# A trunk layer with sixteen experts on one core: two weight parts read one stage earlier, a table read early, the last sums of squares regrouped

## The chip, the core and the metric

The kernel runs on one NeuronCore of a Trainium2 chip. Its metric is the time that the device takes for one execution, in microseconds. A core has five engines with a queue each: TensorE (PE in the profile; PEld is its weight load), VectorE (DVE), ScalarE (ACT), GpSimd (POOL) and SyncE (SP), which here only issues DMA transfers. The engines wait for each other by semaphores.

## The reference

A sequence of 2048 positions of 1024 numbers, all float32, passes one layer. A mixer (three groups of heads side by side, each normalised, then one output product) is added to the input. Then a mixture of experts is added, and the sum is normalised:

```
h = x + mixer(x)
e = two experts of 16 for each position          # best group of four, then best two inside it
y = sum over the two of gate * (silu(xn @ w_gate[e]) * (xn @ w_up[e])) @ w_down[e]   # xn = rms_norm(h)
out = rms_norm(h + y) * final_norm_g
```

An expert's `w_gate` and `w_up` are 1024 x 512, its `w_down` 512 x 1024.

## The kernel before

Products are done in three passes: every float32 operand is split into a rounded high part and the rest, and high x high, high x low and low x high are summed (the three matmuls in a row of each kind).

`phases12` computes the mixer and the routing. A small scheduler written in Python (`Flow`) sets the order of its work when the program is built. The mixer's output product runs over two halves of the positions, each in four chunks of 256 columns; a chunk's split weights lie in a tile `w` of a pool with two buffers, 4416 float32 wide, chunk after chunk. In the fourth chunk (`m == 3`) SP stores every finished tile of h twice, to `hd` and to `hc`. `route` then chooses the experts and sorts the (position, expert) pairs into blocks of 128 of one expert. Its tables (which expert and which ring slots a block uses, how many blocks an expert has, the number of blocks `nb`, the last block `nl`) lie in `tab`.

`moe` runs the blocks. Its engines have an explicit program each, and start together behind a barrier. There are 42 blocks in this run.

- An expert's weights are six parts of 1 MB, numbered over all experts from 0 to 95: parts 0 to 3 of an expert hold gate and up columns, parts 4 and 5 the down rows. SP reads part n into a raw buffer (`raw(n)`). VectorE splits it into one of nine slots of `ring` (L1600 or L1598 the high halves, L1618 or L1616 the low ones), then counts `s_w`. Parts 0 and 1 lie in `stg`, two buffers that `route` fills (L1330) while the mixer ends. Parts 2 to 5 are read after the barrier into slots 6 and 7 of the ring, which are not yet in use. All later parts use the two buffers of `stg` in turn, and the read of part n waits until part n - 2 is split:

```
for n in range(NST, 96):
    if n == 4:
        sp.wait_ge(p_q, 2)
    if n >= 6:
        sp.wait_ge(s_w, n - NST + 1 if n > 7 else n - 5)
```

- TensorE, in step b: reads three numbers of the table (`load`, L1673), multiplies gate and up of block b (L1692, 24 matmuls for each half f of the 512 columns, which wait for the part's `s_w`), transposes the product of block b - 1 (`th`) and the input of block b + 1 (`tx`), both at L1699, and does the down product of block b - 1 (L1731 to L1733). Before the first step it runs 16 and 6 transposes that compute nothing (`warm`, L1666). After the last step it reads three numbers again (L1771, at a place that depends on `nl`) and does the last down product.
- ScalarE moves results out of PSUM, applies silu (`glu`, L1813 and L1814, into `hs` and `hu`), and computes each finished block's normalisation (`newton`, L1860 and on).
- GpSimd gathers a block's rows (L1892), multiplies hs by hu (`hm`, L1910), adds a block's output to `hd` (L1896), reads finished rows back (L1900), multiplies them by `gf` (L1945; `gf` itself is scaled once at L1930) and stores them (L1904).
- The end: after the last step GpSimd copies two index columns (L1951), does a tiny operation (L1955) and reads back the rows of the last two blocks into `ze[0]` and `ze[1]`. VectorE adds the last down product to `ze[0]` in two halves (L1643), ScalarE sums squares in four halves (L1887), first both of `ze[1]`, then both of `ze[0]`, and VectorE turns the sums into factors (from L1645) and scales.

Of the kernel before, what the change touches and what calls it, by code (L numbers as in the profile page):

```python
# [9 lines left out]
F32 = mybir.dt.float32  # L10
F32R = mybir.dt.float32r
# [8 lines left out]
P = 128  # L20
S = 2048
D = 1024
# [122 lines left out]
def phases12(tc, io, hd, hc, tab, gcol, ident, c8, stg):  # L145
# [5 lines left out]
    with ctx:  # L151
# [6 lines left out]
        wp = pool("w", 2)  # L158
# [42 lines left out]
        def wgen():  # L201
            for n in range(len(chunks)):
                raws = load_w_raw(n)
                yield
                while begun[0] < n - 1:
                    yield
                w = wp.tile([P, 2, 8, 276], F32R, name="w")
                for k in range(0, 8, 2):
                    rw_ = raws[k // 4][:, k % 4:k % 4 + 2, :]
                    for j in range(2):  # L210
                        g = col(chunks[n][2], k + j)
                        A.activation(w[:, 0, k + j, 0:256], rw_[:, j], AF.Copy, scale=g)  # L212
                    for j in range(2):
                        stt(w[:, 1, k + j, 0:256], rw_[:, j], col(chunks[n][2], k + j), w[:, 0, k + j, 0:256].bitcast(F32), OP.mult, OP.subtract)
                    yield
                if n in routed:
                    while "rw" not in done:
                        yield
                    G.tensor_copy(w[:, 0, :, 256:276], routed[n])
                    tt(w[:, 1, :, 256:276], routed[n], w[:, 0, :, 256:276].bitcast(F32), OP.subtract, G)  # L220
                wt[n] = w
                if 6 <= n < 14:
                    yield from route_w(n - 6)
                if n == 2:
                    yield from spatial_w()
            done.add("w")
# [859 lines left out]
        def route():  # L1086
# [240 lines left out]
            while stg is not None and len(stg) < NST:  # L1327
                t = c8.tile([P, 2048], F32, name="stg", tag="c8")
                for o, i in stage(io, t, len(stg)):
                    nc.sync.dma_start(out=o, in_=i)  # L1330
                stg.append(t)
# [163 lines left out]
def moe(tc, io, hd, hc, out, tab, gcol, ident, stg):  # L1495
# [5 lines left out]
    with ctx:  # L1501
# [3 lines left out]
        ring = mp.tile([P, RING, 2, 2048], F32R, name="ring")  # L1505
        xg = mp.tile([P, 2, D + 16], F32, name="xg")
        sc = mp.tile([P, 48, 2], F32, name="sc")
# [4 lines left out]
        yb = mp.tile([P, 2, D], F32, name="yb")  # L1512
        gf = mp.tile([P, D], F32, name="gf")
        idf = mp.tile([P, 48], I32, name="idf")
        nw = mp.tile([P, 12], F32, name="nw")
# [4 lines left out]
        ew = mp.tile([P, 6, 2], F32, name="ew")  # L1520
# [9 lines left out]
        s_er = [S_("er%d" % i) for i in range(4)]  # L1530

        raw = lambda n: ring[:, 6 + (n - 2) // 2, n % 2].bitcast(F32) if 2 <= n < 6 else stg[n % NST]
# [25 lines left out]
        with tc.tile_critical():  # L1558
            with nc.Block() as blk:
                @blk.sync  # L1560
                def _(sp):
                    sp.wait_ge(p_q, 1)
                    for n in range(NST, 96):
                        if n == 4:
                            sp.wait_ge(p_q, 2)
                        if n >= 6:
                            sp.wait_ge(s_w, n - NST + 1 if n > 7 else n - 5)
                        if n == RING:
                            sp.dma_start(out=gf, in_=io["final_norm_g"].unsqueeze(0).to_broadcast((P, D))).then_inc(s_gf, 16)
                        for o, i in stage(io, raw(n), n):  # L1570
                            sp.dma_start(out=o, in_=i).then_inc(s_er[n - 2] if n < 6 else s_st[n % NST], 16)

                @blk.vector
                def _(v):
                    nhi = nha = 0
                    for n in range(96):
# [67 lines left out]
                    v.wait_ge(s_es, 4)  # L1644
# [17 lines left out]
                def _(t):  # L1662
                    def warm(n):

                        for _ in range(n):
                            t.transpose(pd[0][:, 0:P], ident, ident)  # L1666
# [78 lines left out]
                    def step(b):  # L1745
                        m = load(b)
# [24 lines left out]
                    m = [t.value_load(meta[0:1, ds(nl * 3 + j, 1)], min_val=0, max_val=(90 if j == 0 else RING - 3)) for j in range(3)]  # L1771
                    t.wait_ge(s_hm, nl * 2 + 2)
                    t.wait_ge(a_ht, nl)
                    th()
                    t.wait_ge(s_hlo, 1)
                    t.wait_ge(a_y, nl)
                    down(m)

                @blk.scalar
                def _(a):  # L1780
# [64 lines left out]
                    def newton(f):  # L1845
# [9 lines left out]
                        if f == 0:  # L1855
                            a.wait_ge(p_k, 3)
                            a.wait_ge(p_q, 1)
# [18 lines left out]
                    if 3 in AH:  # L1876
                        a.wait_ge(s_er[1], 32)
                        hi(3, range(4))
                    chain(a, nb, 0, NBMAX, step)
                    n = 0  # L1880
                    for i in (1, 0):
                        for h in range(2):
                            a.wait_ge(s_zl if i == 0 else s_e[i], 1 + h if i == 0 else 16)
                            if n:
                                a.wait_ge(s_es, n)
                            n += 1
                            a.activation(pj, ze[i][:, h * 512:(h + 1) * 512], AF.Square, accum_out=es[:, h, i:i + 1]).then_inc(s_es, 1)  # L1887

                @blk.gpsimd
                def _(g):  # L1890
# [26 lines left out]
                    g.memset(cmag, float(0x1EF759DF)).then_inc(p_k, 1)  # L1917
                    nb = g.value_load(meta[0:1, 159:160])
# [5 lines left out]
                    g.tensor_copy(nw[:, 7:8], c15).then_inc(p_q, 1)  # L1924

# [24 lines left out]
                    for i in range(2):  # L1950
                        g.tensor_copy(idg[:, i:i + 1], idf[:, ds(nl - i, 1)]).then_inc(p_c, 1)  # L1951
# [4 lines left out]
                    for i in range(2):  # L1956
                        back(ze[i], idg[:, i:i + 1], s_e[i])
                    for i in range(2):
                        g.wait_ge(s_v, fin_v[0] - 1 + i)
                        store(ze[i], idg[:, i:i + 1])  # L1960
# [3 lines left out]
def trunk(tc, io, out):  # L1964
    nc = tc.nc
    with tc.tile_pool(name="outer", bufs=1) as po, tc.tile_pool(name="c8", bufs=2) as c8, tc.tile_pool(name="odr", bufs=1, space=DRAM) as pd:
# [7 lines left out]
        phases12(tc, io, hd, hc, tab, gcol, ident, c8, stg)  # L1974
# [26 lines left out]
```

## Time and profile before

| | us |
|---|---|
| median of 3 runs | 1590.1 |
| the three runs | 1586.15, 1590.1, 1593.86 |
| profiled execution | 1590.12 |
| its span, first to last instruction | 1588.3 |
| TensorE busy | 1489.4 (94% of the span) |
| VectorE busy | 976.4 (61%) |
| ScalarE busy | 865.6 (54%) |
| GpSimd busy | 484.6 (31%) |

The mixer's output product ends about 737 us from the start of the span, the routing about 762 us, and the blocks' steps run from there to about 1553 us. A share of busy time is an average over these stages. What sets the end is read from the chain of waits and from each engine's timeline at the start, in the first steps and at the end of the experts' stage.

### The profile page before, as it was taken

The page shows a single profiled execution, that of the slowest core. Times are in us where ns is not written, and L with a number is a line of the kernel's source. Part 1 is how long each engine was busy: PE and PEld are TensorE (multiplying, and loading weights), DVE is VectorE, ACT ScalarE, POOL GpSimd, SP SyncE. Part 2 cuts the span into 40 slices and gives each one's busy share as a digit, 9 for nine tenths or more (in the row PEclk, how much of TensorE's full clock was granted, in tenths as well). Part 3 has the DMA queues.
Part 4 walks back from the last instruction along what each step waited for, and adds up shares of the span by engine and source line. Part 5 has one row for each costly group of instructions (what it writes and reads, how often), then busy time and mean ns, then how long its engine had stood idle before and what let it go on. Part 6 is the DMA issues. An engine that isn't in the chain of part 4 may idle for free.

```text
span 1588.3 us, 25588 instructions
## 1 busy us (share of the span) xinstructions
PE 1489.4 (94%) x8373; PEld 1283.5 (81%) x8374; DVE 976.4 (61%) x2009; ACT 865.6 (54%) x1915; POOL 484.6 (31%) x400
## 2 busy tenths in 40 slices
PE   7998989999999999996899899999999999999993
PEld 6776888878899989996688678888888888888882
DVE  6588752664642678888888876577888858203001
ACT  6368544687454444311346456665666665666662
POOL 0132000000000000010355545655555555455442
PEclk9999988999999999998899999999999999999996
DMA  6247733213633627607678887778888877434342
GB/s 179 69 80 142 208 104 120 93 54 93 188 99 104 236 81 263 241 27 267 215 226 241 259 253 198 214 214 264 272 222 236 261 220 204 126 75 107 90 116 74
DMA packets 212862, 267.46 MB, mean 168 GB/s; under 512 B 34808, under 2 KB 177344, under 8 KB 212736
## 3 DMA queue, kind: packets, MB, share of 16 engines
q1 hardware_dynamic: 187792, 201.95, 40.3%
q0 software_dynamic: 24672, 62.80, 16.3%
q8 instruction: 78, 1.28, 0.3%
q10 hardware_dynamic: 272, 1.05, 0.2%
q14 instruction: 48, 0.39, 0.1%
HBM read 217.09 MB, written 76.94 MB: 185 GB/s over the span
## 4 chain that ended last, share of the span: by engine, by line
PE 74%; DVE 13%; DMA 4%; ACT 4%; issue 2%; POOL 1%; SPq 0%; DVEq 0%; POOLq 0%; ACTq 0%
PE pg L1692 24%; PE z L90 8%; PE z L92 8%; PE z L91 8%; PE pd L1733 4%; PE pd L1732 4%; PE pd L1731 4%; DMA stg<-in_expert_w_up_dram 3%; DVE ring L1600 2%; PE pt L1699 2%; DVE ring L1618 2%; DVE ht L171 1%; DVE w L171 1%; PE m L924 1%; DVE xT L169 1%
## 5 line engine op out<-in xcount | busy, mean ns | idle before, releaser
L1692 PE MATMUL pg<-ring,xs 128*128 x2016 | 488.3, 395 | 9.7 <-DVE ring L1618 8.0
L1692 PEld LDWEIGHTS pg<-ring,xs 128*128 128x128 f32 x2016 | 378.2, 189 | 89.7 <-issue 11.8
L90 PE MATMUL z<-w,xT 128*128 128x256 f32 (+1 forms) x848 | 250.4, 295 | 5.6 <-DVE ht L171 3.8
L92 PE MATMUL z<-w,xT 128*128 128x256 f32 (+1 forms) x848 | 244.9, 289 | 6.9 <-DVE xT L169 6.9
L91 PE MATMUL z<-w,xT 128*128 128x256 f32 (+1 forms) x848 | 244.6, 288 | 0.0
L1600 DVE TENSOR_SCALAR ring<-stg,gcol 128x512 fp32r<-128x512 f32 x242 | 130.9, 602 | 169.8 <-PE pg L1692 86.7
L1618 DVE SCALAR_TENSOR_TENSOR ring<-stg,gcol,ring 128x512 fp32r<-128x512 f32 x248 | 213.9, 923 | 0.0
L90 PEld LDWEIGHTS z<-w,xT 128*128 128x128 f32 x848 | 164.3, 194 | 9.0 <-issue 5.1
L92 PEld LDWEIGHTS z<-w,xT 128*128 128x128 f32 x848 | 164.1, 194 | 8.2 <-DVE xT L169 8.2
L91 PEld LDWEIGHTS z<-w,xT 128*128 128x128 f32 x848 | 164.5, 194 | 1.4 <-issue 1.4
L1731 PE MATMUL pd<-ring,hh 128*128 x336 | 131.4, 391 | 1.7 <-DVE hh L1637 1.7
L1896 POOL DMA_INDIRECT hd<-yb,tab x41 | 77.5, 1891 | 177.8 <-ACT yb L1835 177.8
L1733 PE MATMUL pd<-ring,hh 128*128 x336 | 131.2, 390 | 0.0
L1732 PE MATMUL pd<-ring,hh 128*128 x336 | 131.2, 390 | 0.0
L1910 POOL TENSOR_TENSOR hs<-hs,hu 128x256 f32<-128x256 f32 x84 | 106.5, 1268 | 50.1 <-ACT hu L1814 47.8
L1945 POOL TENSOR_TENSOR yb<-yb,gf 128x1024 f32<-128x1024 f32 x40 | 116.2, 2905 | 4.7 <-ACT hu L1860 4.7
L171 DVE SCALAR_TENSOR_TENSOR w<-raw,vec,w 128x256 fp32r<-128x256 f32 x176 | 82.0, 510 | 55.4 <-ACT w L212 55.4
L212 ACT ACTIVATE w<-raw,vec 128x256 fp32r<-128x256 f32 x176 | 77.1, 497 | 60.8 <-PE z L92 36.7
L90 PE MATMUL z<-xT,w 128*128 128x512 f32 x256 | 109.8, 429 | 0.2 <-ACT xT L312 0.2
L171 DVE SCALAR_TENSOR_TENSOR ht<-z,rsd,ht 128x256 f32<-128x256 f32 x176 | 85.1, 484 | 30.1 <-PE z L92 22.2
L91 PE MATMUL z<-xT,w 128*128 128x512 f32 x256 | 101.5, 396 | 0.2 <-DVE xT L169 0.2
L92 PE MATMUL z<-xT,w 128*128 128x512 f32 x256 | 101.3, 396 | 0.0
(441 smaller groups left out, 2573.2 us busy)
## 6 DMA issues: line engine op xcount, KB each, us to landing
stg<-in_expert_w_gate_dram SPq DMA_DIRECT2D x62, 512.0 KB
stg<-in_expert_w_up_dram SPq DMA_DIRECT2D x62, 512.0 KB
stg<-in_expert_w_down_dram SPq DMA_DIRECT2D x60, 512.0 KB
raw<-in_w_in_dram SPq DMA_DIRECT2D x48, 256.0 KB
raw<-in_w_out_dram SPq DMA_DIRECT2D x24, 512.0 KB
ht<-in_x_dram SPq DMA_DIRECT2D x16, 512.0 KB
yp<-yTd SPq DMA_DIRECT2D x8, 1024.0 KB
hd<-ht SPq DMA_DIRECT2D x16, 512.0 KB
```

The lines of the kernel that those rows point to most:

```text
L90: nc.tensor.matmul(ps, ah, bh, start=first, stop=False)
L91: nc.tensor.matmul(ps, ah, bl, start=False, stop=False)
L92: nc.tensor.matmul(ps, al, bh, start=False, stop=last)
L171: stt = lambda o, a, s, b, o0, o1: V.scalar_tensor_tensor(out=o, in0=a, scalar=s, in1=b, op0=o0, op1=o1)
L1600: x = v.tensor_scalar(out=ring[:, r, 0, sl], in0=src[:, sl], scalar1=g, scalar2=None, op0=OP.mult)
L1618: x = v.scalar_tensor_tensor(out=ring[:, r, 1, sl], in0=src[:, sl], scalar=g, in1=hi, op0=OP.mult, op1=OP.subtract)
L1692: i = t.matmul(pg[f], xx[j // 2], w[j % 2], start=k == 0 and j == 0, stop=k == 7 and j == 2)
L1731: t.matmul(pd[n], hh[:, 0, kf], w[0], start=kf == 0, stop=False)
L1732: t.matmul(pd[n], hh[:, 0, kf], w[1], start=False, stop=False)
L1733: i = t.matmul(pd[n], hh[:, 1, kf], w[0], start=False, stop=kf == 3)
L1910: g.tensor_tensor(out=o, in0=o, in1=hu[:, f * 256:(f + 1) * 256], op=OP.mult).then_inc(s_hm, 1)
L1945: g.tensor_tensor(out=z, in0=z, in1=gf, op=OP.mult).then_inc(p_z, 1)
```

## The change

It has three parts.

1. The pool of `w` is parted into two pools of one buffer, one of them (`we`) opened outside, so that its memory lives on. When the last chunk of the mixer begins (`h == 1 and m == 3`), the buffer of the chunk before the last is free. ScalarE's queue then issues four transfers that read parts 2 and 3 into it. In `moe`, parts 2 and 3 are taken from there (`early`), parts 4 and 5 are read into ring slot 7, SP begins with part 4, and its wait for `p_q` of 2 is gone. The same memory is later cut into `yb`, `gf`, `hs`, `hu` and small tiles, so ScalarE's first `glu` waits until part 3 is split (`s_w` of 4).
2. TensorE reads the numbers of step 0 and those of the last block before its first `tx`, and runs 8 of the idle transposes into `pt[0]` before its last down product.
3. GpSimd copies the two index columns before its first step, into a place of their own. ScalarE's last squares are three: the first half of `ze[0]`, the whole of `ze[1]` (into the float8 scratch `jb` that `newton` uses), the second half of `ze[0]`. A memset gives the sum that is no longer written.

```diff
-        wp = pool("w", 2)
+        wp = pool("w")
...
-                w = wp.tile([P, 2, 8, 276], F32R, name="w")
+                w = (wp if n % 2 else we).tile([P, 2, 8, 276], F32R, name="w")
...
                 w = chunk(n)
                 n += 1
+                if h == 1 and m == 3:
+
+                    t = we.tile([P, 4416], F32, name="w", tag="w")
+                    for j in range(2):
+                        for o, i in stage(io, t[:, j * 2048:(j + 1) * 2048], 2 + j):
+                            A.dma_start(out=o, in_=i)
+                    stg.append(t)
...
+        early = stg[NST]
...
-        hs = mp.tile([P, 512], F32, name="hs")
-        hu = mp.tile([P, 512], F32, name="hu")
+        yb = cut(2 * D).rearrange("p (a n) -> p a n", a=2)
+        gf = cut(D)
+        hs, hu = cut(512), cut(512)
...
-        raw = lambda n: ring[:, 6 + (n - 2) // 2, n % 2].bitcast(F32) if 2 <= n < 6 else stg[n % NST]
+        raw = lambda n: early[:, (n - 2) * 2048:(n - 1) * 2048] if 2 <= n < 4 else ring[:, 7, n % 2].bitcast(F32) if 4 <= n < 6 else stg[n % NST]
...
-                    for n in range(NST, 96):
-                        if n == 4:
-                            sp.wait_ge(p_q, 2)
+                    for n in range(4, 96):
...
-                        elif n >= NST:
-                            v.wait_ge(s_er[n - 2], 32)
+                        elif n >= 4:
+                            v.wait_ge(s_er[n - 4], 32)
...
-                    v.wait_ge(s_es, 4)
+                    v.wait_ge(s_es, 3)
...
+                    m0 = load(0)
+                    ml = [t.value_load(meta[0:1, ds(nl * 3 + j, 1)], min_val=0, max_val=(90 if j == 0 else RING - 3)) for j in range(3)]
...
-                        m = load(b)
+                        m = load(b) if b else m0
...
-                    m = [t.value_load(meta[0:1, ds(nl * 3 + j, 1)], min_val=0, max_val=(90 if j == 0 else RING - 3)) for j in range(3)]
...
                     th()
+                    warm(8, pt[0][:, 0])
...
-                    down(m)
+                    down(ml)
...
+                        if b == 0 and f == 0:
+                            a.wait_ge(s_w, 4)
...
-                    for i in (1, 0):
-                        for h in range(2):
-                            a.wait_ge(s_zl if i == 0 else s_e[i], 1 + h if i == 0 else 16)
-                            if n:
-                                a.wait_ge(s_es, n)
-                            n += 1
-                            a.activation(pj, ze[i][:, h * 512:(h + 1) * 512], AF.Square, accum_out=es[:, h, i:i + 1]).then_inc(s_es, 1)
+                    a.wait_ge(s_hm, nl * 2 + 2)
+                    for i, h in ((0, 0), (1, None), (0, 1)):
+                        a.wait_ge(s_e[1] if i else s_zl, 16 if i else 1 + h)
+                        if n:
+                            a.wait_ge(s_es, n)
+                        n += 1
+                        if i:
+                            a.activation(jb, ze[1], AF.Square, accum_out=es[:, 0, 1:2], saturate=False).then_inc(s_es, 1)
+                        else:
+                            a.activation(pj, ze[0][:, h * 512:(h + 1) * 512], AF.Square, accum_out=es[:, h, 0:1]).then_inc(s_es, 1)
...
+                    g.wait_ge(p_n, 1)
+                    for i in range(2):
+                        g.tensor_copy(idl[:, i:i + 1], idf[:, ds(nl - i, 1)]).then_inc(p_c, 1)
...
-                    for i in range(2):
-                        g.tensor_copy(idg[:, i:i + 1], idf[:, ds(nl - i, 1)]).then_inc(p_c, 1)
```

The names in the rows of order below are those of the tiles (`ring` for a slot of the ring, `stg` for the two raw buffers, `w` for all that lies in the buffer of `we`). SP's queue at the start of `moe`, before:

```order
L1560 UNCONDITIONAL_BRANCH
L1571 DMA ring<-in_expert_w_gate_dram 128x4x256
L1571 DMA ring<-in_expert_w_up_dram 128x4x256
L1571 DMA ring<-in_expert_w_gate_dram 128x4x256
L1571 DMA ring<-in_expert_w_up_dram 128x4x256
L1571 DMA ring<-in_expert_w_down_dram 128x1024 x4
L1571 DMA stg<-in_expert_w_gate_dram 128x4x256
```

and now:

```order
L1574 UNCONDITIONAL_BRANCH
L1583 DMA ring<-in_expert_w_down_dram 128x1024 x4
L1583 DMA stg<-in_expert_w_gate_dram 128x4x256
L1583 DMA stg<-in_expert_w_up_dram 128x4x256
L1583 DMA stg<-in_expert_w_gate_dram 128x4x256
L1583 DMA stg<-in_expert_w_up_dram 128x4x256
```

The four transfers of parts 2 and 3 have left SP's queue, and the down parts 4 and 5 stand first.

TensorE between the barrier and its first gate and up matmuls (`pt` is the transposed input of block 0, `pd` takes the idle transposes, TENSOR_LOAD reads a table number), before:

```order
L1699 MATMUL pt_7846<-ident,xg 128x128 x4
L1699 MATMUL pt_7847<-ident,xg 128x128 x4
L1666 MATMUL pd_7850<-ident 128x128 x6
L1704 MATMUL pt_7846<-xs,nid 128x512
L1704 MATMUL pt_7847<-xs,nid 128x512
L1673 TENSOR_LOAD tab
L1673 ISA x2
L1673 TENSOR_LOAD tab
L1673 ISA x2
L1673 TENSOR_LOAD tab
L1673 ISA x2
L1683 REGISTER_ALU
```

and now (the three reads of `m0` stand just ahead of these rows):

```order
L1688 TENSOR_LOAD tab
L1688 ISA x3
L1688 TENSOR_LOAD tab
L1688 ISA x3
L1688 TENSOR_LOAD tab
L1688 ISA x2
L1714 MATMUL pt_7846<-ident,xg 128x128 x4
L1714 MATMUL pt_7847<-ident,xg 128x128 x4
L1678 MATMUL pd_7850<-ident 128x128 x6
L1719 MATMUL pt_7846<-xs,nid 128x512
L1719 MATMUL pt_7847<-xs,nid 128x512
L1698 REGISTER_ALU
```

All six reads stand ahead of the first transposes, none between them and the first product.

GpSimd's end, from the store of the last block that a step finishes, before:

```order
L1904 DMA out_dram<-yb,idf 2048x1024
L1552 UNCONDITIONAL_BRANCH
L1951 ISA
L1951 COPY tab<-idf 128x1
L1951 ISA
L1951 COPY tab<-idf 128x1
L1954 REGISTER_ALU
L1955 TENSOR_TENSOR nw<-nw 128x1
L1900 DMA stg<-hd,tab 128x1024 x2
```

and now:

```order
L1921 DMA out_dram<-w 2048x1024
L1566 UNCONDITIONAL_BRANCH
L1973 REGISTER_ALU
L1974 TENSOR_TENSOR w<-w 128x1
L1917 DMA stg<-hd,w 128x1024 x2
```

The two copies are gone from between the store and the reading back.

## Rows read from the trace of the kernel before

**Rows 1.** The page: its span, and the chain that ended last by engine.
```profile
span 1588.3 us, 25588 instructions
...
PE 74%; DVE 13%; DMA 4%; ACT 4%; issue 2%; POOL 1%; SPq 0%; DVEq 0%; POOLq 0%; ACTq 0%
```

**Rows 2.** The chain of waits in order of time: start us, length us, step.
```profile
765.29 7.77 DMA ring<-in_expert_w_up_dram
...
799.93 6.84 DMA stg<-in_expert_w_up_dram
...
920.39 3.03 PE pg L1692 x12
928.86 5.44 PE pg L1692 x24
...
947.23 5.44 PE pg L1692 x24
```

**Rows 3.** VectorE's timeline: start us, length us, line, operation; in brackets idle before.
```profile
763.62 5.44 DVE L1618 SCALAR_TENSOR_TENSOR ring<-stg,gcol,ring 128x512 fp32r<-128x512 f32 x8
773.08 1.67 DVE L1600 TENSOR_SCALAR ring<-ring,gcol 128x512 fp32r<-128x512 f32 x4 [4.02 <-DMA ring<-in_expert_w_up_dram]
...
788.51 3.11 DVE L1600 TENSOR_SCALAR ring<-stg,gcol 128x512 fp32r<-128x512 f32 x4
...
799.76 2.37 DVE L1600 TENSOR_SCALAR ring<-stg,gcol 128x512 fp32r<-128x512 f32 x4 [1.26 <-DMA stg<-in_expert_w_up_dram]
...
806.87 5.30 DVE L1600 TENSOR_SCALAR ring<-stg,gcol 128x512 fp32r<-128x512 f32 x4 [2.09 <-DMA stg<-in_expert_w_up_dram]
...
915.44 1.68 DVE L1600 TENSOR_SCALAR ring<-stg,gcol 128x512 fp32r<-128x512 f32 x4 [1.14 <-DMA stg<-in_expert_w_up_dram]
```

**Rows 4.** TensorE's timeline, the first steps.
```profile
768.66 1.09 PE L1699 MATMUL pt<-ident,xg 128*128 128x128 f32 x8 [2.08 <-DMA xg<-hc,tab]
...
772.66 7.36 PE L1692 MATMUL pg<-ring,xs 128*128 x24 [1.66 <-issue]
...
783.94 8.33 PE L1692 MATMUL pg<-ring,xs 128*128 x36
```

**Rows 5.** SP's timeline: the first reads of parts 6 and 7.
```profile
774.56 0.48 SPq L1571 DMA_DIRECT2D stg<-in_expert_w_gate_dram  x1
...
775.84 3.14 SPq L1571 DMA_DIRECT2D stg<-in_expert_w_gate_dram  x1
```

**Rows 6.** GpSimd's timeline, the first steps.
```profile
782.40 6.78 POOL L1910 TENSOR_TENSOR hs<-hs,hu 128x256 f32<-128x256 f32 x1 [9.67 <-ACT hu L1814]
...
807.29 3.42 POOL L1930 TENSOR_SCALAR gf<-gf 128x1024 f32<-128x1024 f32 x1
...
826.03 2.95 POOL L1945 TENSOR_TENSOR yb<-yb,gf 128x1024 f32<-128x1024 f32 x1
```

**Rows 7.** Stretches of 5 us: busy time by engine, granted clock, DMA share, GB/s.
```profile
740.00:745.00 5.00, 0.00 (x0) 0.00 (x0) 4.35 (x23) 0.00 (x0) 0.00 (x0) 0.50 1.03 419
...
750.00:755.00 5.00, 0.79 (x6) 0.32 (x6) 4.66 (x16) 0.00 (x0) 1.63 (x5) 0.50 0.00 0
```

**Rows 8.** All engines' timeline, the end.
```profile
1553.65 1.05 ACT L1860 ACTIVATE hu<-yb 128x1024 fp8e4<-128x1024 f32 x1
...
1554.59 0.19 ACT L1860 ACTIVATION_READ_ACCUMULATOR hu<-yb 128x1 f32 x1
...
1556.40 1.09 PE L1699 MATMUL ph<-ident,hs 128*128 128x128 f32 x4 [3.38 <-issue]
...
1561.09 0.32 POOL L1951 COPY tab<-idf 128x1 int32 x2
...
1561.65 0.19 POOL L1955 TENSOR_TENSOR nw<-nw 128x1 f32<-128x1 f32 x1 [0.25 <-POOL tab L1951]
...
1568.13 0.60 ACT L1887 ACTIVATE pj<-stg 128x512 f32<-128x512 f32 x1 [8.89 <-DMA stg<-hd,tab]
...
1571.33 0.16 DVE L1645 SCALAR_TENSOR_TENSOR ew<-ew 128x2 f32<-128x2 f32 x1 [4.26 <-ACT pj L1887]
```

More of the change, by code (lines that the diff above doesn't have):

```diff
@@ L1326, in route @@
             digits(slice(0, 8))
-            while stg is not None and len(stg) < NST:
+            for n in range(NST):
                 t = c8.tile([P, 2048], F32, name="stg", tag="c8")
-                for o, i in stage(io, t, len(stg)):
+                for o, i in stage(io, t, n):
                     nc.sync.dma_start(out=o, in_=i)
-                stg.append(t)
+                stg.insert(n, t)
             yield from half(1)
@@ L1505, in moe, with cut @@
         ring = mp.tile([P, RING, 2, 2048], F32R, name="ring")
+        early = stg[NST]
+        off = [0]
+        def cut(n):
+            off[0] += n
+            return early[:, off[0] - n:off[0]]
         xg = mp.tile([P, 2, D + 16], F32, name="xg")
-        sc = mp.tile([P, 48, 2], F32, name="sc")
         xs = mp.tile([P, 2, 2, 8, P], F32R, name="xs")
-        hs = mp.tile([P, 512], F32, name="hs")
-        hu = mp.tile([P, 512], F32, name="hu")
+        yb = cut(2 * D).rearrange("p (a n) -> p a n", a=2)
+        gf = cut(D)
+        hs, hu = cut(512), cut(512)
         hh = mp.tile([P, 2, 4, P], F32R, name="hh")
[L1512 to L1515, printed above, removed]
+        sc = cut(96).rearrange("p (b j) -> p b j", j=2)
+        idf = cut(48).bitcast(I32)
+        nw = cut(12)
+        idl = cut(2).bitcast(I32)
         jb = hu[:, 0:256].bitcast(mybir.dt.float8e4)
@@ L1519, in moe @@
         ya = nw[:, 8:10]
-        ew = mp.tile([P, 6, 2], F32, name="ew")
+        ew = cut(12).rearrange("p (a b) -> p a b", b=2)
         es, et, ev, ey = ew[:, 0:2], ew[:, 2], ew[:, 3], ew[:, 4:6]
@@ L1529, in moe @@
         s_w, s_hi, s_ha, p_q, p_c = S_("w"), S_("hi"), S_("ha"), S_("pq"), S_("pc")
-        s_er = [S_("er%d" % i) for i in range(4)]
-        raw = lambda n: ring[:, 6 + (n - 2) // 2, n % 2].bitcast(F32) if 2 <= n < 6 else stg[n % NST]
+        s_er = [S_("er%d" % i) for i in range(2)]
+        raw = lambda n: early[:, (n - 2) * 2048:(n - 1) * 2048] if 2 <= n < 4 else ring[:, 7, n % 2].bitcast(F32) if 4 <= n < 6 else stg[n % NST]
         s_u = [S_("u%d" % i) for i in range(6)]
@@ L1570, in _ @@
                         for o, i in stage(io, raw(n), n):
-                            sp.dma_start(out=o, in_=i).then_inc(s_er[n - 2] if n < 6 else s_st[n % NST], 16)
+                            sp.dma_start(out=o, in_=i).then_inc(s_er[n - 4] if n < 6 else s_st[n % NST], 16)
                 @blk.vector
@@ L1662, in _, with warm @@
                 def _(t):
-                    def warm(n):
+                    def warm(n, ps=pd[0][:, 0:P]):
                         for _ in range(n):
-                            t.transpose(pd[0][:, 0:P], ident, ident)
+                            t.transpose(ps, ident, ident)
                     warm(16)
@@ L1855, in newton @@
                         if f == 0:
-                            a.wait_ge(p_k, 3)
+                            a.wait_ge(p_k, 4)
                             a.wait_ge(p_q, 1)
@@ L1956, in _ @@
                     for i in range(2):
-                        back(ze[i], idg[:, i:i + 1], s_e[i])
+                        back(ze[i], idl[:, i:i + 1], s_e[i])
                     for i in range(2):
                         g.wait_ge(s_v, fin_v[0] - 1 + i)
-                        store(ze[i], idg[:, i:i + 1])
+                        store(ze[i], idl[:, i:i + 1])
                     g.wait_ge(s_o, nl * 16 + 16)
@@ L1965, in trunk @@
     nc = tc.nc
-    with tc.tile_pool(name="outer", bufs=1) as po, tc.tile_pool(name="c8", bufs=2) as c8, tc.tile_pool(name="odr", bufs=1, space=DRAM) as pd:
+    with tc.tile_pool(name="outer", bufs=1) as po, tc.tile_pool(name="c8", bufs=2) as c8, tc.tile_pool(name="we", bufs=1) as we, tc.tile_pool(name="odr", bufs=1, space=DRAM) as pd:
         tab = po.tile([P, 368], F32, name="tab")
```

8 lines of the change are left out of this document (3 added, 5 removed).

## The prediction, made before the changed kernel was run

> **What bounds the kernel now.** I read the page's chain by engine first: TensorE has 74% of it [rows 1], so only what moves TensorE's last matmuls, or what follows them, can move the end. The chain in order of time then shows a stretch that isn't TensorE's. From 765.29, the transfer that brings part 2, to 920.39 it runs through DMA and VectorE, and TensorE is on it again only from there [rows 2]. Block 8 begins at 928.86 and block 9 at 947.23, so an unhindered block takes 18.37 us [rows 2]. In the row at 783.94 the last 24 of 36 matmuls belong to block 1, which so begins at about 783.94 + 12/36 x 8.33 = 786.7 [rows 4]. Seven unhindered blocks would bring block 8 to 786.7 + 7 x 18.37 = 915.3. It starts 13.6 us later: the supply of split weights sets that start, and TensorE has 13.6 us to spare ahead of it. From block 8 to the last step TensorE is its own bound.
>
> VectorE's timeline shows how the supply begins late. Parts 0 and 1 are split by 763.62 + 5.44 = 769.06; then VectorE waits 4.02 us for part 2 [rows 3]. Later it waits again and again for a read (1.26, 2.09, 1.14 us [rows 3]), since a buffer's next read is issued only when its part is split: read, split, read, split, in two interleaved chains. A part that is split later makes the part two on later by as much.
>
> At the end, ScalarE waits for the rows of `ze[1]` until 1568.13, sums four halves, and VectorE goes on at 1571.33 [rows 8].
>
> **The change part by part.**
>
> *Parts 2 and 3 read early.* VectorE's wait of 4.02 us goes [rows 3]. It splits parts 2 and 3 from 769.06 on. A part takes 1.67 for its four high operations and, by the row of eight, 4/8 x 5.44 = 2.7 for its low ones [rows 3], 4.3 in all, so part 3 is done near 777.6 instead of 781.6. What is late next? Parts 4 and 5 are now issued when part 2 was, near 765, and took over part 2's place in the DMA queues; part 2 came 7.77 us after its second transfer was issued [rows 2], so part 4 is there by 773 and needed at 777.6. The reads of parts 6 and 7, issued at 774.56 and 775.84 before [rows 5], now wait only for parts 0 and 1 to be split (766.4 and 769.1); they are needed from 784.5 (788.51 [rows 3] less 4.0) and 4.3 later. So no read is late until part 8, whose read waits for part 6 to be split and moves with it. From there each part moves by the same 4.0 us, if its split takes as long as before.
>
> That last condition is the uncertain one. VectorE and GpSimd hold each other up. Where GpSimd's scaling of `gf` runs (3.42 us from 807.29 [rows 6]), VectorE's four operations on part 9 take 5.30 us [rows 3] instead of 1.67: 3.63 us lost. The four on part 6 take 3.11 [rows 3], 1.44 more. GpSimd's multiplication by `gf` (2.95 us at 826.03 [rows 6]) comes once for each of TensorE's steps. These go by TensorE's clock, and the supply moves against it, so other parts will be hit. Lower bound: the next such holds take all 4.0 us back, 0. Upper bound: parts 6 and 9 escape theirs and no other part meets one: 4.02 + 1.44 + 3.63 = 9.1 us. I take 4.0: VectorE is busy most of this stretch, so a hold that leaves one part mostly finds another.
>
> What the edit adds: four DMA issues on ScalarE's queue, at the nearest rows 0.48 to 3.14 us each [rows 5], 2 to 13 us. They stand behind the last squares of the chunk before, wait for the same matmuls, and ahead of the first squares of the last chunk. Those sums are needed only after four tiles; were the cover gone, the factors for the routing would be late by what remains of it. The 2.1 MB take about 5 us of transfers at the 419 GB/s of that stretch, and the DMA engines then stand at 0.00 from 750 to 755 [rows 7]: ten microseconds and more of cover before the barrier near 762. I count 0; the bounds are 0 and 3 us lost. The new wait of the first `glu` for part 3 (777.6) is over before the matmuls that it waits for anyway, which were done at 772.66 + 7.36 = 780.0 [rows 4] and will be 1.66 earlier at most; behind it stand only that step's evacuations. 0.
>
> *TensorE's table reads.* The three reads before the first product cost the 1.66 us of issue in front of it [rows 4]. Six reads now lie ahead of the first transposes, which wait 2.08 us for the gathered rows anyway [rows 4]. Bounds: 1.66 us gained; or, if each read costs a third of the 3.38 us at the end [rows 8], 6 x 1.13 - 2.08 = 4.7 us lost. Neither counts: block 8 waits for weights, and TensorE still has 13.6 - 4.0 = 9.6 us to spare. At the end the 3.38 us of issue go [rows 8], and the eight idle transposes (1.1 us, like the eight at 768.66 [rows 4]) lie beside VectorE's two operations on `hh`. But the end doesn't wait for TensorE: ScalarE waits 8.89 us for the rows read back [rows 8]. 0, and what would be lost if that cover were gone is the same 1.1 us.
>
> *GpSimd's copies.* They leave the path to the reading back: 1561.65 - 1561.09 = 0.56 us [rows 8]. In their new place GpSimd waits 9.67 us for its next work [rows 6], so they cost nothing there.
>
> *Three squares.* Four halves took 1571.33 - 1568.13 = 3.20 us, 0.80 each [rows 8]. The whole of a tile takes, as in `newton`, 1554.59 + 0.19 - 1553.65 = 1.13 us [rows 8], about 1.17 to the next. The first half of `ze[0]` comes during the wait for `ze[1]`. Left after that wait: 1.17 + 0.80 = 1.97, so 1.23 us are gained. With the copies 1.8 us; bounds 1.0 (the first half of `ze[0]` isn't done in time, 0.80 less) and 2.6 (the last read back comes earlier by as much).
>
> Sum: 4.0 + 1.8 = 5.8 us. Made against the profiled execution, 1590.12 us, whose span is 1588.3 [rows 1] with 1.8 us around it; the median of the three runs is the same 1590.1. 1590.1 - 5.8 = **1584.3 us**.
>
> **The rivals.**
>
> *Given back* (0.14): the supply's start is earlier, but GpSimd's holds, which come once in 18.37 us, catch VectorE one part on and take the 4 us again by block 7. For it: the holds at 807.29 and 826.03 are one step apart [rows 6], and three splits with their reads take about as long, so the same phase can return. Against it: they would have to cost more than before, where part 9 alone already lost 3.63. Time: 1590.1 - 1.8 = 1588.3.
>
> *Out of step* (0.22): the opposite. The 4 us carry part 9 past the scaling of `gf` (its four operations would lie at 803 to 804.5, before 807.29), and that loss isn't met elsewhere: 4.02 + 3.63 + 1.8 = 9.4, so 1580.7. TensorE's 13.6 us allow it. Against it: part 10 then lies where part 9 was.
>
> *GpSimd starved* (0.06), the slower side. GpSimd's product of hs and hu at 782.40 took 6.78 us [rows 6] while VectorE worked without a gap. Without the wait for part 2, VectorE has no gap from 763 until it waits for part 8, near 799.76 - 1.26 - 4.0 = 794.5 [rows 3]. If both products of block 0 wait for that gap, they end some 2.5 us behind it, near 797, and TensorE, which needs them for `th` near 783.94 + 8.33 - 1.66 = 790.6 [rows 4], stands for 6.4 us. That is within the 9.6 us to spare. The rival decides from 9.6 us on and passes the time before at 9.6 + 5.8 = 15.4: three blocks so delayed give 19.2 us and 1590.1 + 3.8 = 1593.9, four give 1600.3. The Trainium skill speaks for the mechanism: in SBUF — State Buffer, "Who interferes with whom", VectorE's operations in a two-port mode or with two inputs in SBUF and GpSimd's share one port pair as an exclusive lock, and whoever comes second waits for the whole instruction. By that rule the trace's 6.78 us and VectorE's lengthened operations are the same lock seen from both sides; the trace agrees, though it also shows GpSimd getting in after some operations and not after others, which the rule leaves open.
>
> *Not what it says* (0.04): the early reads land late or hold the barrier. For it nothing but that ScalarE's queue is shared; against it the idle DMA engines after 750 [rows 7]. Up to 3 us lost and the 4 us gained: about 1587.
>
> **How the numbers follow.** Forecast 0.54, given back 0.14, out of step 0.22, starved 0.06, not what it says 0.04. Less than 0.5%, here 8 us, can't be told from no change. The forecast's own range is 1581.5 to 1587.0 (2.5 us either way of what the holds may shift). With the first two rivals, 1588.3 and 1580.7, and the 3.9 us that single runs lie from their median, I give 1579.0 to 1589.8. Faster by over 0.5% means below 1582.1: all of out of step and a tenth of the forecast, 0.27. Slower by over 0.5%: the worse half of starved, 0.03. The rest, 0.70, is within.
>
> **What would show it.** The steps are right if VectorE has no idle time between parts 1 and 2; if part 3 is split near 777.6 and part 27, on which block 7 waits, about 4 us before TensorE's 920.39 [rows 2]; if block 8 starts near 924.8 and the blocks after it still take 18.37; and if, at the end, VectorE's first small operation comes about 2.0 us after the wait for `ze[1]`. The forecast is wrong if block 8 starts less than 1.5 us earlier or more than 7, or if TensorE's first wait in block 1 is for GpSimd and grows beyond 9.6 us.

## The result, and the profile after

The changed kernel takes **1600.8 us** (median of 5 runs, 1598.6 to 1602.5) against 1590.1: a ratio of 1.0068, 95% interval 1.0053 to 1.0084. It is 10.7 us slower where 5.8 us less was forecast. The profiled execution took 1598.6 us.

The page of after: its span, and the chain that ended last by engine, answering to [rows 1].

```profile
span 1596.9 us, 25606 instructions
...
PE 74%; DVE 14%; DMA 4%; ACT 4%; issue 2%; POOL 1%; SPq 0%; DVEq 0%; POOLq 0%; ACTq 0%
```

The span is 8.6 us longer and TensorE's share is the same. So I looked where its steps stand. The chain of waits of after, answering to [rows 2] (start us, length us, step); the last 24-matmul row belongs to block 41, the last block:

```profile
924.68 5.57 PE pg L1707 x24
943.43 5.61 PE pg L1707 x24
...
1544.77 5.60 PE pg L1707 x24
1573.38 4.51 DMA stg<-hd,w
```

The same view of before, block 41:

```profile
1534.66 5.44 PE pg L1692 x24
```

Block 8 starts at 924.68 instead of 928.86 [rows 2], 4.2 us earlier. From there to block 41 after takes 620.1 us and before 605.8: 18.79 us a block instead of 18.36, in each of 33 blocks, 14.3 us in all. The last block's start to the end of the span takes 52.1 instead of 53.6, 1.5 less. -4.2 + 14.3 - 1.5 = 8.6: the difference of the spans. The whole loss lies in TensorE's own pace: 24 gate matmuls take 5.60 us instead of 5.44 [rows 2], 233 ns each instead of 227, with no wait between them. The granted clock of this stretch is 1.00 in both traces, the level of 2.4 GHz. It is the third number from the end in the rows of stretches, before and then after:

```profile
1000.00:1540.00 540.00, 540.00 (x2559) 451.25 (x2558) 292.38 (x377) 338.21 (x768) 293.11 (x205) 1.00 0.67 187
```

```profile
1000.00:1540.00 540.00, 540.00 (x2504) 441.08 (x2503) 289.40 (x377) 332.17 (x753) 281.71 (x202) 1.00 0.66 185
```

Which matmuls? Groups of PE instructions by line and form, 1000 to 1540 us (count, busy us, mean ns of one; a matmul's end overlaps the next one's start). Before:

```profile
L1692 PE MATMUL pg<-ring,xs 128*128 x1416 | 339.0, 392 | 0.0
L1732 PE MATMUL pd<-ring,hh 128*128 x236 | 91.8, 389 | 0.0
...
L1699 PE MATMUL pt<-ident,xg 128*128 128x128 f32 x232 | 30.1, 273 | 0.0
L1704 PE MATMUL pt<-xs,nid 128*128 128x512 f32 x58 | 17.9, 389 | 0.0
...
L1704 PE MATMUL ph<-hh,nid 128*128 128x512 f32 x29 | 11.3, 389 | 0.0
```

After:

```profile
L1707 PE MATMUL pg<-ring,xs 128*128 x1392 | 340.8, 396 | 0.0
L1746 PE MATMUL pd<-ring,hh 128*128 x226 | 89.3, 395 | 0.0
...
L1714 PE MATMUL pt<-ident,xg 128*128 128x128 f32 x232 | 30.1, 273 | 0.0
L1719 PE MATMUL pt<-xs,nid 128*128 128x512 f32 x58 | 18.1, 394 | 0.0
...
L1719 PE MATMUL ph<-hh,nid 128*128 128x512 f32 x29 | 11.4, 392 | 0.0
```

All matmuls of 512 columns are slower by 3 to 6 ns, on lines that the change didn't touch; the transposes (273 ns) are not. These matmuls read `ring` as the moving operand (or `xs`, `hh`), and `xs`, `hh` or `nid` as the stationary one. The diff moves all four: the early tile, 17664 bytes a partition, now stands in front of them, and `sc`, `hs`, `hu`, `yb`, `gf`, `idf` and `nw` left the places between them. The matmuls take the same operands by the same code; only the addresses differ.

The rest went for the most part as the prediction had it. VectorE's timeline of after, answering to [rows 3] (in brackets idle before):

```profile
762.30 5.45 DVE L1630 SCALAR_TENSOR_TENSOR ring<-stg,gcol,ring 128x512 fp32r<-128x512 f32 x8
767.67 1.66 DVE L1612 TENSOR_SCALAR ring<-w,gcol 128x512 fp32r<-128x512 f32 x4
...
803.35 4.40 DVE L1612 TENSOR_SCALAR ring<-stg,gcol 128x512 fp32r<-128x512 f32 x4 [4.37 <-DMA stg<-in_expert_w_up_dram]
```

The wait of 4.02 us for part 2 is gone. Part 9, at 803.35, still loses 4.40 - 1.67 = 2.7 us, and VectorE waits 4.37 us for its read, where it waited 2.09 before [rows 3]. TensorE's first steps, answering to [rows 4]; the row of `th` has no wait in front:

```profile
769.36 5.75 PE L1707 MATMUL pg<-ring,xs 128*128 x24
...
787.43 0.60 PE L1714 MATMUL ph<-ident,w 128*128 128x128 f32 x4
```

And the end, all engines, answering to [rows 8]:

```profile
1576.57 0.60 ACT L1904 ACTIVATE pj<-stg 128x512 f32<-128x512 f32 x1 [6.78 <-DVE stg L1655]
...
1577.92 1.06 ACT L1902 ACTIVATE w<-stg 128x1024 fp8e4<-128x1024 f32 x1 [0.63 <-DMA stg<-hd,w]
...
1579.91 0.16 DVE L1657 SCALAR_TENSOR_TENSOR w<-w 128x2 f32<-128x2 f32 x1 [2.78 <-ACT pj L1904]
```

From the wait for `ze[1]` to VectorE's first small operation: 1.99 us, before 3.20 [rows 8].

### The profile page after: what moved, and what is told of

It is laid out like the page before. It is cut to its first block, busy times and chain, and to the rows that moved or that the text cites. A ratio compares the mean times of both kernels' runs of the same rounds, so it can differ in the third digit from the quotient of the medians.

```text
span 1596.9 us, 25606 instructions
## 1 busy us (share of the span) xinstructions
PE 1503.0 (94%) x8381; PEld 1282.2 (80%) x8382; DVE 975.6 (61%) x2009; ACT 865.4 (54%) x1913; POOL 474.3 (30%) x401
## 4 chain that ended last, share of the span: by engine, by line
PE 74%; DVE 14%; DMA 4%; ACT 4%; issue 2%; POOL 1%; SPq 0%; DVEq 0%; POOLq 0%; ACTq 0%
PE pg L1707 24%; PE z L90 8%; PE z L92 8%; PE z L91 8%; PE pd L1748 4%; PE pd L1747 4%; PE pd L1746 4%; DMA stg<-in_expert_w_up_dram 3%; DVE ring L1630 3%; DVE ring L1612 3%; PE pt L1714 2%; DVE ht L171 1%; DVE w L171 1%; DVE xT L169 1%; PE pt L1719 1%
## 5 line engine op out<-in xcount | busy, mean ns | idle before, releaser
L1707 PE MATMUL pg<-ring,xs 128*128 x2016 | 496.4, 398 | 7.5 <-DVE ring L1630 7.5
L1612 DVE TENSOR_SCALAR ring<-stg,gcol 128x512 fp32r<-128x512 f32 x242 | 141.6, 646 | 186.9 <-PE pg L1707 92.9
L1630 DVE SCALAR_TENSOR_TENSOR ring<-stg,gcol,ring 128x512 fp32r<-128x512 f32 x248 | 199.8, 865 | 0.0
L1746 PE MATMUL pd<-ring,hh 128*128 x336 | 132.8, 395 | 0.8 <-DVE hh L1649 0.8
L1748 PE MATMUL pd<-ring,hh 128*128 x336 | 132.7, 395 | 0.0
L1747 PE MATMUL pd<-ring,hh 128*128 x336 | 132.7, 395 | 0.0
L1913 POOL DMA_INDIRECT hd<-w,tab x41 | 71.6, 1746 | 190.4 <-ACT w L1852 190.4
L1966 POOL TENSOR_TENSOR w<-w 128x1024 f32<-128x1024 f32 x40 | 117.3, 2932 | 3.1 <-ACT w L1877 2.9
L1927 POOL TENSOR_TENSOR w<-w 128x256 f32<-128x256 f32 x84 | 103.2, 1228 | 48.8 <-ACT w L1831 47.8
```

What stands on the lines that cost most here:

```text
L1612: x = v.tensor_scalar(out=ring[:, r, 0, sl], in0=src[:, sl], scalar1=g, scalar2=None, op0=OP.mult)
L1630: x = v.scalar_tensor_tensor(out=ring[:, r, 1, sl], in0=src[:, sl], scalar=g, in1=hi, op0=OP.mult, op1=OP.subtract)
L1707: i = t.matmul(pg[f], xx[j // 2], w[j % 2], start=k == 0 and j == 0, stop=k == 7 and j == 2)
L1746: t.matmul(pd[n], hh[:, 0, kf], w[0], start=kf == 0, stop=False)
L1747: t.matmul(pd[n], hh[:, 0, kf], w[1], start=False, stop=False)
L1748: i = t.matmul(pd[n], hh[:, 1, kf], w[0], start=False, stop=kf == 3)
```

## The experiments

Two theories at first. *Place*: the 512-column matmuls go by where the tiles that TensorE reads begin in SBUF. *Program*: something in the changed instructions slows TensorE, for instance the table numbers it now holds in registers to the end. The starts below are the tiles' addresses in the built programs, in bytes of a partition, modulo 256. Every slice that a matmul reads begins a multiple of 512 bytes behind its tile's start, so the tiles' starts stand for the operands'. "24 gates" is the chain's row of 24 gate matmuls, "block" the mean from block 8 to block 41; times are medians, those with a star of one run.

| kernel | ring | xs | hh | nid | 24 gates, us | block, us | time, us |
|---|---|---|---|---|---|---|---|
| before | 96 | 96 | 96 | 96 | 5.44 | 18.36 | 1590.1 |
| after | 96 | 224 | 224 | 224 | 5.60 | 18.79 | 1600.8 |
| before, 256 bytes in front of ring | 96 | 96 | 96 | 96 | 5.45 | 18.36 | 1589.8 |
| before, 416 bytes in front of ring | 0 | 0 | 0 | 0 | 5.44 | 18.36 | 1590.4 |
| after, early tile at the other end | 96 | 224 | 224 | 224 | 5.61 | 18.81 | 1600.7 |
| the same, xs and hh ahead of xg | 96 | 96 | 96 | 224 | 5.44 | 18.41 | 1585.8 |
| after, xg behind nid | 96 | 96 | 96 | 96 | 5.45 | 18.36 | 1584.9 |
| before, stationary moved | 96 | 224 | 160 | 96 | 5.58 | 18.79 | 1607.7* |
| before, moving moved | 224 | 96 | 96 | 96 | 5.58 | 18.74 | 1608.5* |
| before, all at 224 | 224 | 224 | 224 | 224 | 5.44 | 18.37 | 1590.3 |
| before, all at 160 | 160 | 160 | 160 | 160 | 5.44 | 18.45 | 1592.2* |
| before, 32 bytes in front of xs | 96 | 128 | 128 | 128 | 5.60 | 18.80 | 1603.8* |
| before, 256 bytes in front of xs | 96 | 96 | 96 | 96 | 5.44 | 18.41 | 1593.1* |

**Is it the place, and which operand's?** Four kernels, two of either program:

```
+gap = mp.tile([P, 64], F32, name="gap")      # or 104: 256 or 416 unused bytes
 ring = mp.tile([P, RING, 2, 2048], F32R, name="ring")
```

> Place (the 512-column matmuls go by where the tiles that TensorE reads begin in SBUF): this is the kernel before with an unused tile of 256 bytes a partition in front of ring, so ring, xs and hh begin 352 bytes past a multiple of 512 (before 96, after 352, 480 and 480). A block takes 18.79 us instead of 18.36, a gate matmul 233.5 ns instead of 226.7, and the time is 1590.1 + 34 x 0.43 = 1604.7 us. Program (something in the changed instructions slows TensorE, wherever the tiles lie): a block takes 18.36 us and the time is 1590.1.

> The kernel before with an unused tile of 416 bytes in front of ring: ring, xs and hh begin at multiples of 512. Place: no row shows this start; if a start within 512 bytes counts, the best is here, and a gate matmul takes between 213.3 ns (512 columns at 2.4 GHz) and 226.7 ns, a block between 17.4 and 18.36 us. Program: 226.7 ns, 18.36 us, 1590.1 us.

Both are as fast as before (ratios 0.9995, 0.9979 to 1.0011, and 1.0010, 0.9997 to 1.0022). *Place*, as put there (a start within 512 bytes), was wrong for these.

```
-tc.tile_pool(name="we", bufs=1) as we
+tc.tile_pool(name="we", bufs=1, side="right") as we
```

> The changed kernel with its tile for the early parts at the other end of SBUF: ring is back at the byte where it was before (96 past a multiple of 512), xs and hh begin 224 past one (before 96, after 480). Place, by the moving operand (ring): a block takes 18.36 us and the time is 1600.8 - 34 x 0.43 = 1586.2 us. Place, by the stationary operands (xs and hh): a block differs from 18.36, by how much no row shows. Program: a block takes 18.79 us and the time is 1600.8.

```
-xg = mp.tile([P, 2, D + 16], F32, name="xg")
 xs = mp.tile([P, 2, 2, 8, P], F32R, name="xs")
 hh = mp.tile([P, 2, 4, P], F32R, name="hh")
+xg = mp.tile([P, 2, D + 16], F32, name="xg")
```

> As the one before it in this set, and xs and hh stand ahead of xg, so that ring, xs and hh all begin 96 bytes past a multiple of 512, as before the change. Place, by either operand: a block takes 18.36 us and the time is 1586.2 us. Program: 18.79 us and 1600.8.

The first, with `ring` back at its old byte, is slow (1.0057, 1.0033 to 1.0082); the second, with the same instructions and only the order of three tiles changed, is fast (0.9982, 0.9967 to 0.9997). *Program* falls. The chain's block 41, first kernel and then second:

```profile
1552.19 5.61 PE pg L1707 x24
```

```profile
1532.61 5.44 PE pg L1707 x24
```

In the second, `nid` still begins 128 bytes off the others, and the matmuls that read it are slow, 396 and 404 ns instead of 389; its block takes 18.41, not 18.36:

```profile
L1707 PE MATMUL pg<-ring,xs 128*128 x1414 | 339.6, 392 | 0.0
...
L1719 PE MATMUL pt<-xs,nid 128*128 128x512 f32 x58 | 18.3, 396 | 0.0
L1719 PE MATMUL ph<-hh,nid 128*128 128x512 f32 x29 | 11.7, 404 | 0.0
```

**An absolute start, or a distance?** So far every slow kernel had its stationary operands at 224. Either that start is bad for them, or it is the distance from the moving operand's.

```
-xg = mp.tile([P, 2, D + 16], F32, name="xg")
 ...
 nid = mp.tile([P, P], F32R, name="nid")
+xg = mp.tile([P, 2, D + 16], F32, name="xg")
```

> The changed kernel with one tile's allocation moved: xg behind nid, so that xs, hh and nid (the stationary operands) begin 96 bytes past a multiple of 256 instead of 224; ring (the moving one) stays where the change put it. Stationary start alone: gate, down and nid matmuls take 226.7 ns, a block 18.36 us, block 8 begins near 924.5 and the time is 1600.8 - 34 x 0.43 = 1586.2 us or, from the last run of the set before (1585.75, whose nid matmuls were slow, 0.05 us a block), 1584.0. Distance between two operands' starts (slow unless ring and xs, or xs and nid, lie some multiple of 256 apart): gate matmuls 226.7, but nid ones 232 as in the changed kernel, where xs and nid were a multiple of 256 apart too. Program: 18.79 us, 1600.8 us.

Unused tiles in the kernel before: 128 bytes in front of `xs`, 192 of `hh`, 192 of `nid`; then 128 in front of `ring` and 128 of `xs`:

> The kernel before with unused tiles that move only the stationary operands: xs begins 224 past a multiple of 256, hh 160, nid 96, ring 96 as before. Stationary start: gate matmuls 233.5 ns, nid ones 226.7, down ones between 226.7 and 237.5 (no row for 160), a block 18.36 + 48/72 x 0.43 = 18.65 us or up to 18.79, and the time 1590.1 + 34 x 0.29 = 1600.0 us or up to 1604.7. Program: 226.7 ns everywhere, 18.36 us, 1590.1 us. Distance: as stationary start for the gate matmuls; the run after it in this set tells these two apart.

> The kernel before with unused tiles that move only the moving operand: ring begins 224 past a multiple of 256; xs, hh and nid 96 as before. Stationary start: 226.7 ns, 18.36 us, 1590.1 us. Moving start or distance between ring's and xs's starts: gate and down matmuls 233.5 ns, a block 18.79 us, 1604.7 us.

The changed kernel with one line moved is faster than before and after: 1584.9 us, a ratio to before of 0.9968 (0.9955 to 0.9981). The expectation from the distance missed one point here. It had the matmuls that read `nid` stay slow, and they are not:

```profile
L1719 PE MATMUL pt<-xs,nid 128*128 128x512 f32 x58 | 17.9, 389 | 0.0
```

By this run alone the stationary start would do. But both forms of the kernel before, whose instructions are its own, are slow. Groups by form, first the one with its stationary operands moved (down matmuls: 64 bytes apart), then the one with `ring` moved:

```profile
L1695 PE MATMUL pg<-ring,xs 128*128 x1379 | 336.8, 396 | 0.0
L1734 PE MATMUL pd<-ring,hh 128*128 x232 | 91.9, 396 | 0.0
```

```profile
L1694 PE MATMUL pg<-ring,xs 128*128 x1380 | 336.9, 396 | 0.0
L1734 PE MATMUL pd<-ring,hh 128*128 x232 | 91.8, 396 | 0.0
```

The moving operand alone does it too: a rule for the stationary start alone falls. Then 128 or 64 bytes in front of `ring`, which moves all four alike, and 32 in front of `xs`:

> The kernel before with an unused tile of 128 bytes in front of ring: ring, xs, hh and nid all begin 224 past a multiple of 256. Distance (TensorE is slowed where the starts of the operands that it reads together do not lie some multiple of 256 bytes apart): gate and down matmuls 226.7 ns, a block 18.36 us, 1590.1 us. Absolute start (any operand that begins 224 past a multiple of 256 slows it): 233.5 ns or more, a block 18.79 us or more, 1604.7 us or more.

> The same with 64 bytes: ring, xs, hh and nid all begin 160 past a multiple of 256, where hh alone at 160 made the down matmuls 233.4 ns. Distance: 226.7 ns, 18.36 us, 1590.1 us. Absolute start: 233.4 ns, 18.8 us, 1604.7 us.

> The kernel before with 32 unused bytes in front of xs: ring begins 96 past a multiple of 256; xs, hh and nid 128. Distance: slow, since 32 is no multiple of 256: gate and down matmuls above 226.7 ns, at 233.5 a block of 18.79 us and 1604.7 us. Absolute start with only 160 to 224 slow: 226.7 ns, 18.36 us, 1590.1 us.

With all four at 224 (1.0008, 0.9989 to 1.0026), or all at 160, where single operands were slow, the matmuls are fast; with 32 bytes between `ring` and `xs` they are slow. The chain's block 41 of the three, in this order:

```profile
1532.44 5.44 PE pg L1693 x24
```

```profile
1536.75 5.44 PE pg L1693 x24
```

```profile
1547.66 5.60 PE pg L1693 x24
```

So for the gate and down matmuls the distance decides. Last, 256 bytes in front of `xs`, to tell a multiple of 256 from one of 512:

> The kernel before with 256 unused bytes in front of xs: ring begins 96 past a multiple of 512; xs and hh 352, a distance of 256 between the moving and the stationary operands. If only a multiple of 512 is free of the loss: gate and down matmuls near 233 ns, a block 18.8 us, 1604.7 us. If a multiple of 256 is enough: 226.7 ns, 18.36 us, 1590.1 us.

The row of 24 takes 5.44 us, as block 41 shows: a multiple of 256 is enough.

```profile
1537.39 5.44 PE pg L1693 x24
```

(The blocks of 18.41 here and 18.45 with all at 160 hold waits around the `nid` matmuls of single blocks; their other matmuls are as in before.)

**What the forecast's own terms are worth.** Two kernels take one part back out of the fast form (xg behind nid). Without the early reading, parts 2 and 3 go into `ring` after the barrier as before:

```
-raw = lambda n: early[...] if 2 <= n < 4 else ring[:, 7, n % 2] ...
+raw = lambda n: ring[:, 6 + (n - 2) // 2, n % 2] if 2 <= n < 6 else ...
-for n in range(4, 96):
+for n in range(NST, 96):
```

> The changed kernel with xg allocated behind nid (its fast placing), and the early reading undone: parts 2 and 3 are read as before, after the barrier, into ring. If the early reading is worth what was forecast: block 8 begins about 4 us later than in the changed kernel, near 928.5, and the time is 1584.9 + 2.9 (block 8 of the fast placing began at 925.8) to 4.0 = 1587.8 to 1588.9. If it is hidden or given back: block 8 near 925.8, 1584.9.

Without the three parts of the last sums:

```
-for i, h in ((0, 0), (1, None), (0, 1)):
+for i in (1, 0):
+    for h in range(2):
```

> The same placing, with the early reading, and the last sums taken of four halves again instead of three parts. If the three parts are worth what was forecast: from ScalarE's wait for the rows of ze[1] to VectorE's first small operation 3.2 us instead of 1.99, and 1584.9 + 1.2 = 1586.1 us. If something else ends last there: 1584.9.

The wait came out as expected: the end, all engines, of the kernel with halves shows 1567.20 - 1564.01 = 3.19 us where the fast form has 1.99.

```profile
1564.01 0.60 ACT L1901 ACTIVATE pj<-stg 128x512 f32<-128x512 f32 x1 [8.46 <-DMA stg<-hd,w]
...
1567.20 0.16 DVE L1657 SCALAR_TENSOR_TENSOR w<-w 128x2 f32<-128x2 f32 x1 [4.43 <-ACT pj L1901]
```

From block 41's start to the end it has 53.2 us, the fast form 51.9. That is 1.3 us for the three parts. Its time was 1588.3 (ratio 0.9985, 0.9968 to 1.0002), 2.2 above the 1586.1 expected; the kernel before was 1.7 us slower in this set too (1591.2 against 1589.4 in that of the fast form).

Without the early reading the first run missed: VectorE waits for part 2 again, yet block 8 began at 925.2, and the time was 1586.9 (0.9969, 0.9949 to 0.9990), the same ratio as the fast form's. VectorE's timeline of it:

```profile
771.88 1.68 DVE L1611 TENSOR_SCALAR ring<-ring,gcol 128x512 fp32r<-128x512 f32 x4 [3.69 <-DMA ring<-in_expert_w_up_dram]
```

So both went once more, on one chip:

> The changed kernel in its fast placing once more, beside the next run on the same chip, which lacks the early reading alone. Early reading worth what its traces so far show (block 8 at 923.8 to 925.8 in four kernels that read early, 926.1 to 928.7 in five that don't, 3.0 us between the means): about 1585 us, 3 us under the next run, block 8 near 924.7. Given back: the same time as the next run.

> The same without the early reading, whose first profile had block 8 at 925.0 and whose time lay 2 us above the fast placing's by medians from two different calls. Worth 3 us: block 8 near 927.7 this time, 1588 us. Given back: block 8 near 925 again, 1585 us.

1584.6 us with the early reading (0.9969, 0.9956 to 0.9982), 1587.4 without (0.9986, 0.9972 to 1.0000). Block 8, in the chains of the two:

```profile
922.44 5.44 PE pg L1707 x24
```

```profile
927.24 5.45 PE pg L1706 x24
```

Block 8's start scatters between single profiles of one program by as much as the part is worth: 925.97 and 922.44 in the two with the early reading, 925.18 and 927.24 in the two without. In the kernel with the early tile at the other end, which reads early too, it is 931.40; the expectation above left that one out of its 923.8 to 925.8, and the two slow forms of before with the stationary or the moving operands shifted (931.9 and 934.0) out of its 926.1 to 928.7. So the part's worth is taken from the times, not from block 8. Over the four sets of 12 runs the means differ by 3.0 us (95% interval 1.5 to 4.5, from the scatter of the runs).

## Why the prediction was wrong

**The step that failed** is "block 8 starts near 924.8 and the blocks after it still take 18.37". Its first half held (924.68). The second took it as given that a matmul on an untouched line keeps its duration. The diff showed the tiles of every one of these matmuls in new places, and the sum had no term for that, nor had a rival or the range. It is worth 33 x 0.433 = 14.3 us: 0.43 us over the 72 matmuls with `ring` in a block are 6 ns each. The prediction itself gave the reason why nothing covers it: from block 8 on TensorE is its own bound.

**Parts 2 and 3 early: right.** VectorE has no gap between parts 1 and 2. Block 8 came 4.2 us earlier in after; 1.3 of that was there already at VectorE's row of eight (762.30 against 763.62 [rows 3]) and about as much was lost again on the way. Where the loss sits shows in VectorE's rows: part 8 begins 5.8 us earlier (793.97 against 799.76 [rows 3]), part 9, after the longer wait for its read, 3.5 earlier (803.35 against 806.87).

```profile
793.97 1.88 DVE L1612 TENSOR_SCALAR ring<-stg,gcol 128x512 fp32r<-128x512 f32 x4 [0.87 <-DMA stg<-in_expert_w_up_dram]
```

Taken back alone, the part cost 3.0 us (1.5 to 4.5); 4.0 was forecast. (The 4.3 us for a part's split are 1.67 + 2.7 = 4.4 by the prediction's own terms; the starts in after lie 4.24 apart.)

**The last squares and GpSimd's copies: right in size.** The wait to VectorE's operation takes 1.99 us, "about 2.0" forecast. The last block's start to the end: 53.6 us before, 51.9 in the fast form, 1.7 less; 1.8 forecast. The squares alone are worth 1.3 of it, by the run with halves; no run takes the copies alone back, so the rest is theirs by the forecast only.

**TensorE's table reads: as forecast, but not tested alone.** The 1.66 us of issue in front of the first product is gone; that nothing came of it fits the sum, and no run takes this part back.

**The rivals.** *Given back* was about a quarter true (1.0 of 4.0 us; the interval allows nothing to 2.5). *Out of step* fell: part 9 did not pass its hold. *GpSimd starved*, the only rival on the slower side, is not why after is slower: TensorE's first `th`, at 787.43, waits for nothing there. But what it describes does happen: the profile of the kernel with the early tile at the other end, whose instructions are after's, shows it. There GpSimd's gather takes 14.46 us (1.27 in after) and its next operation 6.91 (0.59), and that ends where VectorE first has a gap, at 793. The chain of waits runs through these two, and TensorE's first `th` waits 6.37 us for GpSimd's product; the rival had 6.4. The chain, TensorE's row and a row of VectorE:

```profile
771.85 14.46 POOL xg L1909
...
786.37 6.91 POOL w L1941
```

```profile
796.62 1.12 PE L1714 MATMUL ph<-ident,w 128*128 128x128 f32 x4 [6.37 <-POOL w L1927]
```

```profile
829.95 1.68 DVE L1612 TENSOR_SCALAR ring<-stg,gcol 128x512 fp32r<-128x512 f32 x4 [6.91 <-PE pd L1748]
```

TensorE begins block 2 at 812.38 instead of after's 800.59, 11.8 us later. With 9.6 us to spare, block 8 would be 2.2 us late; it comes at 931.40 instead of 924.68, 6.7 late. The spare time was read as free, but a late TensorE holds the supply up too: at 829.95 VectorE waits 6.91 us for it to release a slot of the ring. That execution took 1606.0 us; of the seven executions of this kernel one more took 1606.9, the others 1597.8 to 1601.7. How often it happens is not known. After itself was slower for a reason that no case had. *Not what it says* fell with the first two steps.

With the tiles' distances mended the same change takes 1584.9 and, in the second set, 1584.6 us; the forecast was 1584.3. The early reading's 3.0 us and the end's 1.7 make 4.7 instead of 5.8, and against before in the same sets the gain is 4.6 and 5.9 us, so that the agreement to half a microsecond is partly luck. What broke the forecast was a side effect of the allocation.

## What to carry to other kernels

Where a diff adds, removes or resizes a tile, write down the starts of the operands of the busiest matmuls before and after it, and keep the moving and the stationary ones a multiple of 256 bytes apart where they are, as here, fp32r and 512 columns wide (nothing else was tried); here the order of four allocations was worth 16 us of 1600, three times the change itself. When a kernel is slower than its steps explain, compare the pace of untouched lines in a stretch where nothing waits, before looking for a new wait. A range made from the bounds of the edits holds only if everything that the diff moves has a bound in it, tiles too.

## What the runs showed of the hardware

With operands of type fp32r at 2.4 GHz, the gate and down matmuls of 512 columns came every 226.7 ns in their rows where the starts of moving and stationary operand lay a multiple of 256 bytes apart (0 and 256 modulo 512), and every 232 to 234 ns on average where 32, 64 or 128 were left over modulo 256. Common starts of 0, 96, 160 and 224 (modulo 256) were alike. In after the spacing of the gate matmuls alternates between 229 and 237 ns.

Why is not shown. Rows of after's last block show when the two are read: the load of the next weights (PEld) begins with the running matmul.

```profile
1571.37 0.40 PE L1747 MATMUL pd<-ring,hh 128*128 x1
1571.37 0.19 PEld L1748 LDWEIGHTS pd<-ring,hh 128*128 128x128 f32 x1
1571.61 0.40 PE L1748 MATMUL pd<-ring,hh 128*128 x1
1571.61 0.19 PEld L1746 LDWEIGHTS pd<-ring,hh 128*128 128x128 f32 x1
```

That the two reads meet in SBUF is therefore likely, but only argued. The Trainium skill, in SBUF — State Buffer, "A bandwidth-pool intuition that's wrong (but worth ruling out)", gives weight loads a second, independent read port beside the moving operand's. The runs don't bear this out as it stands: with the same instructions a block takes 18.36 or 18.8 us by how the two starts lie to each other, which two reads that never meet would not by themselves explain. They don't show where the two meet. Whether a matmul meets its own weights' load or the next one's is open too: where `nid` alone was off by 128, slow rows lay on both sides of the matmuls that read it. Nor does a matmul's own pair explain all: in after `xs`, `hh` and `nid` all begin at 224, and the matmuls that read `nid` still take 392 and 394 ns; with `ring` at 224 too they take 389:

```profile
L1705 PE MATMUL pt<-xs,nid 128*128 128x512 f32 x58 | 17.9, 389 | 0.0
```

So a matmul beside slow ones can be slow though its own operands begin alike.
